# Regrouping attention products, rounded sums on GpSimd and first weights on two queues in a fp32 hybrid trunk

## The chip, the cores and the metric

The kernel runs on one core of a Trainium2 chip. The metric is the device time of one execution in microseconds (us); the median of several runs stands for the kernel. All numbers of the input and the output are fp32.

## The reference

The reference is a trunk of two layers on a sequence of 512 tokens of width 1024. Each layer mixes tokens, adds the scaled input, normalizes, and then does the same with a convolutional feed-forward network (FFN). Layer 0 mixes with a gated delta rule (GDN, six heads of 128) and a dilated sliding-window attention (SWA, three groups of four heads of 64); layer 1 with a differential attention and gated linear attention (GLA, four heads).

```python
def step(state, inp):                                  # gated delta rule, per chunk
    delta = u_n - einsum('bhck,bhkv->bhcv', w_n, state)
    o_n = einsum(qd_n, state) + einsum('bhij,bhjv->bhiv', qk_n, delta)
    state = gl_n[..., None, None] * state + einsum(kd_n, delta)
o_a = rms_norm(o_a, norm_w) * silu(z_a)
...
s = einsum(qb, kb) * dh ** -0.5 + bias                  # dilated branch, per group
p = exp(s - max(s)); o = (p / sum(p)) @ vb; lse = max + log(sum)
o = sum over the three groups of softmax(lse) * o
...
o_n = einsum(q_n * exp(b_n), state) + einsum('bhij,bhjv->bhiv', attn, v_n)   # GLA, per chunk
```

## The kernel before

**Products.** A big fp32 product (projections, FFN, output) is made of three products of rounded parts: a high part in the type fp32r and the rest ('lo'), x_hi w_hi + x_lo w_hi + x_hi w_lo, each a TensorE instruction on a 128 x 128 weight tile and 512 columns. ACT casts the weight's high part ('wh<-wr'), DVE subtracts the rest ('wl<-wr,wh'). Small products of the mixers are plain fp32, for which TensorE executes two instructions each.

**Order.** The core's engines each work through a queue in order. In the mixers the order is made by a planner: projections go out in a fixed sequence (EVEN_SEQ, L90), and between each three of their matmuls (`tile_of`, L371; `by_token`, L397) `poll` may let one of several generators ("chains") issue its next step. A chain gives control back with `yield`; the planner charges each step with rough durations per engine and holds a chain until its result should be there (`issue`). A `yield FREE` makes the chain ready once TensorE's part of the step is done. All small operations issued through the chains carry line L159 in the trace; they are told apart by the names of their tiles.

**What the change touches.**
- START (L93) is the order of the first DMA transfers: eight pieces of the input x on SyncE's queue (SP), and between them pieces of the first two weight units (0 is the narrow gate unit U_AB, 1 the first projection) on ACT's queue. In `setup` (from L221) ACT issues all five weight pieces in program order after a copy of one column (tile 'idle') that loads ACT's function table; the casts of x and of the first weights follow.
- `Scratch` (L166) hands out working tiles of 128 x 512; a tile is allocated when it is first asked for.
- `gdn_chunks` (L1157): for each head and each of four chunks, the state product, the output 'o', its square 'sq' (ACT), 'sq' plus the term 'dt' (GpSimd), its rounded copy 'hi' (ACT, L1198), and the rest 'lo' (GpSimd, L1199). 'hi' and 'lo' later go into the product that gives the mean of squares (`gdn_mean`, tile 'pm').
- `swa_pair` (L1247), for each of two pairs of heads: score products (64 rows deep) into a PSUM tile 'sps' of their own each, a reduction on DVE that adds the bias and takes the maximum, control given back after each; the maxima transposed ('rows', 'pmx'), combined over the groups and negated ('negm', 24 columns); all 24 exponentials on ACT; then, group by group, the transposes of the probabilities ('pt') and the value products into 'po' (128*64 in the trace, "PV" below), control given back after each of four blocks.
- `gla_pair`, the loop that fills 'po': for each chunk the product of 'qe' with the state (64 rows) and the product of the attention 'ats' with v (128 rows).

PSUM tiles for these small products come from a pool of four.

Of the kernel before, what the change touches and what calls it, by code (L numbers as in the profile page):

```python
# [9 lines left out]
F32 = mybir.dt.float32  # L10
# [7 lines left out]
P = 128  # L18
S = 512
# [39 lines left out]
for _n, _w in (("ident", 128), ("maskT", 128), ("nm1", 32), ("i32", 32), ("lm", 4 * 32), ("scan", 512),  # L59
# [30 lines left out]
EVEN_SEQ = "h0 h1 h2 h3 h4 h5 q00 v0 q01 v1 q02 v2 q10 q11 q12 z0 z1 z2 z3 z4 z5"  # L90
ODD_SEQ = "0D12G3abcd"

START = (("x", 0, 1), (0, 0, 4), ("x", 1, 2), (1, 0, 2), ("x", 2, 3), (1, 2, 5), ("x", 3, 4), (0, 4, 8), ("x", 4, 5),  # L93
         ("x", 5, 6), (1, 5, 8), ("x", 6, 7), ("x", 7, 8))
WARM = 8
LEAD = 3
AHEAD = 2
# [68 lines left out]
class Scratch:  # L166


    def __init__(self, t, pool, n, more=None):
        self.t, self.pool, self.free, self.of = t, pool, list(range(n)), {}  # L170
        if more is not None:
            self.free += [(k, more) for k in range(more.shape[1])]

# [21 lines left out]
class Trunk:  # L195
# [14 lines left out]
    def setup(self):  # L210
        nc, tc, ctx = self.nc, self.tc, self.ctx
        self.keep = ctx.enter_context(tc.tile_pool(name="keep", bufs=1))
        self.wp = ctx.enter_context(tc.tile_pool(name="wp", bufs=1))
        self.psd = ctx.enter_context(tc.tile_pool(name="psd", bufs=4, space=PSUM))
        self.pss = ctx.enter_context(tc.tile_pool(name="pss", bufs=4, space=PSUM))
        keep = self.keep
        self.h = keep.tile([P, KD, S], F32, name="h")
        self.xh = keep.tile([P, KD, S], F32R, name="xh")
        self.xl = keep.tile([P, KD, S], F32R, name="xl")
        first = [(u, self.wtiles()) for u in (U_AB, U_AB + 1)]  # L220

        self.ones = keep.tile([P, P], F32, name="ones")
        nc.gpsimd.memset(self.ones, 1.0 / P)
        idle = keep.tile([P, 1], F32, name="idle")
        tc.keep_in_program_order(nc.scalar.copy(out=idle, in_=self.ones[:, 0:1]))
        for what, a, e in START:
            if what == "x":
                nc.sync.dma_start(self.h[:, a, :], self.xt[:, a, :])
            else:

                u, w = first[what]
                n = 64 if u in NARROW else P
                tc.keep_in_program_order(nc.scalar.dma_start(w[0][:, a * n : e * n], self.wts[u][:, a * n : e * n]))
        self.par = keep.tile([P, _NP], F32, name="par")
        self.con = keep.tile([P, _NCC], F32, name="con")

        warm = self.sps("warm")
        for _ in range(WARM):
            nc.tensor.matmul(warm[:, 0:P], lhsT=self.ones, rhs=self.ones, start=True, stop=True)
        self.onesL = keep.tile([P, P], F32, name="onesL")  # L240
        nc.gpsimd.memset(self.onesL, 1.0 / D)
        self.onesP, self.onesK = (keep.tile([P, P], F32R, name=f"ones{i}") for i in "PK")
        for x, n in ((self.onesP, P), (self.onesK, 512)):
            nc.vector.tensor_scalar(out=x, in0=self.ones, scalar1=P / n, scalar2=None, op0=ALU.mult)
        self.cst = keep.tile([P, 3], F32, name="cst")
        self.one, self.lneps, self.gdneps = (self.cst[:, i : i + 1] for i in range(3))
        nc.gpsimd.memset(self.one, 1.0)
        nc.gpsimd.memset(self.lneps, LN_EPS)
        self.rep = tc.dram_tile([4, P, L_TAB], F32, name="rep")
        self.chains, self.rec, self.asked = [], [], {}  # L250
        self.V, self.A = Eng(self, "DVE", nc.vector), Eng(self, "ACT", nc.scalar)
        self.G, self.T = Eng(self, "POOL", nc.gpsimd), Eng(self, "PE", nc.tensor)
        self.enter(EVEN)
        for what, a, e in START:
            if what == "x":
                hi, lo = self.xh[:, a, :], self.xl[:, a, :]
                nc.scalar.copy(out=hi, in_=self.h[:, a, :])
                nc.vector.tensor_tensor(out=lo, in0=self.h[:, a, :], in1=hi.bitcast(F32), op=ALU.subtract)
            else:
                u, w = first[what]  # L260
                self.split(u, *w, nc.scalar, nc.vector, slice(a * P, e * P))
        for u, w in first:
            self.pre[u] = w[1:]
        for u in (U_AB + 2, U_AB + 3):
            self.ask(u)
        nc.sync.dma_start(self.par, self.par_d)
        nc.sync.dma_start(self.con, self.con_d)
        self.ident = self.c("ident")
# [483 lines left out]
    def even(self):  # L752
# [8 lines left out]
        def t1(n, w, bufs):  # L761
            return mp.tile([P, w], F32, name=self.nm(n), tag=n, bufs=bufs)

        self.enter(EVEN)
        g = {"zero": t1("zero", 1, 1)}
        seq = EVEN_SEQ.split()
# [390 lines left out]
    def gdn_chunks(self, hd, kt, cols, xf, ready, g, o, t1):  # L1157
# [15 lines left out]
        for c in range(NCH):  # L1173
# [21 lines left out]
            A.activation(out=ch(sq, c), in_=po, func=AF.Square)  # L1195
            st = sn

            G.tensor_tensor(out=ch(sq, c), in0=ch(sq, c), in1=ch(g["dt"][hd], c), op=ALU.add)  # L1198
            A.copy(out=ch(hi, c).bitcast(F32R), in_=ch(sq, c))  # L1199
            G.tensor_tensor(out=ch(lo, c).bitcast(F32R), in0=ch(sq, c), in1=ch(hi, c), op=ALU.subtract)  # L1200
            yield 0
        X.put(xf, vp, kt, kd, de, at, qe, sq)
# [44 lines left out]
    def swa_pair(self, pair, taken, vts, bg, o, mp, t1):  # L1247
# [12 lines left out]
        for g in range(3):  # L1260
            while len(taken) < 2 * g + 2 or X.room() < 5 or not self.bias:
                yield None
            q, k = taken[2 * g : 2 * g + 2]
            for hh in range(2):
                r = slice(64 * hh, 64 * hh + 64)
                hd = 2 * pair + hh
                tiles = []
                for n in range(NCH):
                    w = 256 if g == 0 and n > 0 else P
                    if n == 0 or (g == 0 and n == 2):  # L1270
                        while X.room() < 1:
                            yield None
                        x = X.get("sc")
                        held.append(x)
                        off = 0
                    dst = x[:, off : off + w]
                    off += w
                    bias = bg[0][:, hd, 256 - w : 256] if g == 0 else bg[g][:, hd, :]
                    k0 = n * P + P - w
                    ps = self.sps("sps")  # L1280
                    if g == 0:
                        m = max(0, 256 - w)
                        self.scores(ps[:, : w + m], q, k, hh, slice(n * P, (n + 1) * P), slice(k0, k0 + w + m))
                    else:
                        T.matmul(ps[:, :w], lhsT=q[r, n * P : (n + 1) * P], rhs=k[r, k0 : k0 + w], start=True, stop=True)
                    ci = hh * 12 + g * NCH + n
                    V.tensor_tensor_reduce(out=dst, in0=ps[:, :w], in1=bias, scale=0.125, scalar=-3e38,
                                           op0=ALU.add, op1=ALU.max, accum_out=mx[:, ci : ci + 1])
                    tiles.append((dst, k0, w))
                    yield FREE  # L1290
                sc[g, hh] = tiles
            X.put(*(q + k[0] + k[1] if g == 0 else [q, k]))

        def rows(cols, rw):

            pr = self.sps("rows")
            T.transpose(out=pr[0:24, 0:P], in_=cols, identity=self.ident)
            tr = t1("tr", P, 2)
            V.tensor_copy(out=tr[0:24, :], in_=pr[0:24, 0:P])
            for hh in range(2):  # L1300
                G.dma_start(rw[hh : hh + 1, :], tr[12 * hh : 12 * hh + 12, :])
# [12 lines left out]
        combine(rw, ALU.max, mrow)  # L1314
        yield 0
        pm = self.sps("pmx")
        for g in range(3):
            for n in range(NCH):
                src = perm(mrow[0:2, :])[:, n, :] if g else mrow[0:2, n * P : (n + 1) * P]
                T.transpose(out=pm[:, (g * NCH + n) * 2 : (g * NCH + n) * 2 + 2], in_=src, identity=self.ident[0:2, 0:2])  # L1320
        X.put(mrow)
        nm = t1("negm", 24, 2)
        V.tensor_scalar(out=nm, in0=pm[:, 0:24], scalar1=-1.0, scalar2=None, op0=ALU.mult)
        ls = t1("ls", 24, 2)
        for g in range(3):
            for hh in range(2):
                for n in range(NCH):
                    ci = (g * NCH + n) * 2 + hh
                    li = hh * 12 + g * NCH + n
                    dst, k0, w = sc[g, hh][n]  # L1330
                    A.activation(out=dst, in_=dst, func=AF.Exp, bias=nm[:, ci : ci + 1], accum_out=ls[:, li : li + 1])
                yield 0 if g == 0 and hh == 1 else FREE
        po = self.sps("po")
        for g in range(3):
            while len(vts[g]) < 2:
                yield None
            pts = {}
# [19 lines left out]
            for n in range(NCH):  # L1357
                for i in range(len(pts[0, n])):
                    for hh in range(2):
# [4 lines left out]
                        else:  # L1364
# [1 line left out]
                        vt, f = (vts[g][pair], kb * P) if g else (vts[g][kb // 2], kb % 2 * HS + P * pair)  # L1366
                        T.matmul(dst, lhsT=vt[:, f + 64 * hh : f + 64 * hh + 64], rhs=src,
                                 start=(g == 0 and n == 0 and i == 0), stop=(g == 2 and n == NCH - 1))
                yield FREE
            X.put(*temps)  # L1370
        X.put(*held)
        if pair:
# [172 lines left out]
    def gla_pair(self, pr, cs, qk, vts, gm, o, t1, done):  # L1545
# [122 lines left out]
        yield 0  # L1668
        for hh in range(2):
            po = self.sps("po")  # L1670
            for n in range(NCH):
                if n:
                    T.matmul(ch(po, n), lhsT=qe[rr[hh], n * P : (n + 1) * P], rhs=sts[n][rr[hh]], start=True, stop=False)
                T.matmul(ch(po, n), lhsT=ch(ats[hh], n), rhs=ch(vt[n], 2 * pr + hh), start=(n == 0), stop=True)
            ss = t1("gss", NCH, 4)
            for n in range(NCH):
                A.activation(out=ch(ats[hh], n), in_=ch(po, n), func=AF.Square, accum_out=ss[:, n : n + 1])
# [325 lines left out]
```

## Time and profile before

| | before |
|---|---|
| median of 3 runs | 1410.34 us (1410.32 to 1410.57) |
| the profiled execution | 1412.89 us |
| its span in the trace | 1411.1 us |
| stages in the trace (us) | start 0 to 18; even mixer 18 to 374; its output product 374 to 430; FFN 430 to 798; odd mixer 798 to 1004; its output product 1004 to 1045; FFN 1045 to 1411 |

The profile was taken in one execution on the chip. PE is TensorE's matmul, DVE VectorE, ACT ScalarE, POOL GpSimd, SP SyncE. L12 is line 12 of the kernel; `out<-in` are the program's names of the tiles. In the timelines a row is: start, duration, engine, line, operation, tiles, shape, count of instructions in a row, and in brackets the idle time before with what ended it. Matmuls are pipelined, so that their durations overlap; the distance of two starts says how long one occupies the engine.

### The profile page before, as it was taken

The numbers are of one execution on the slowest core, as the hardware profiler recorded it, in microseconds if no ns is written. First come the engines' busy times: TensorE is split into PE (matmuls) and PEld (weight loads), VectorE is DVE, ScalarE is ACT, GpSimd is POOL, SyncE is SP. The second block draws the span as 40 slices with busy tenths as digits, with TensorE's granted clock in tenths as the row PEclk, the third lists the DMA queues.
The fourth block names the chain that finished last, engine by engine and source line by source line (L and its number), as shares of the span: only waits on it lengthen the run. The fifth ranks groups of instructions, "written<-read, shape, count | busy, mean of one in ns | idle before, by whom it ended". The sixth has DMA issues, their size and how long they took to land.

```text
span 1411.1 us, 22721 instructions
## 1 busy us (share of the span) xinstructions
PE 1385.7 (98%) x9050; PEld 1151.2 (82%) x9050; DVE 839.3 (59%) x1635; ACT 673.5 (48%) x1285; POOL 179.8 (13%) x237
## 2 busy tenths in 40 slices
PE   8999999999999999999999999999999999999997
PEld 6878787777798888888888977878898888888886
DVE  6876744544586555555243797777776555553354
ACT  6644433644857344434132755557565344432133
POOL 2103012011023111111010310000131111110010
PEclk9999999999999999999999999999999999999998
DMA  7434112121342322323233313211303322223221
GB/s 248 144 111 149 47 61 75 36 73 61 98 128 76 99 95 97 98 95 100 96 98 98 88 61 105 75 46 60 120 31 119 99 96 95 99 95 100 91 73 60
DMA packets 41457, 130.42 MB, mean 92 GB/s; under 512 B 4637, under 2 KB 9485, under 8 KB 41352
## 3 DMA queue, kind: packets, MB, share of 16 engines
q1 hardware_dynamic: 35584, 119.05, 26.1%
q10 hardware_dynamic: 4184, 4.92, 1.2%
q0 software_dynamic: 1584, 5.00, 1.1%
q8 instruction: 71, 1.16, 0.3%
q14 instruction: 34, 0.28, 0.1%
HBM read 126.76 MB, written 5.29 MB: 94 GB/s over the span
## 4 chain that ended last, share of the span: by engine, by line
PE 83%; DVE 6%; ACT 5%; DMA 3%; issue 2%; POOL 1%; ACTq 0%; DVEq 0%; POOLq 0%
PE pd L487 18%; PE pd L488 18%; PE pd L489 17%; PE pd L371 16%; PE pd L397 3%; DMA wr<-wts 2%; PE pc L159 1%; PE po L159 1%; PE sps L159 1%; PE pz L159 1%; PE py L159 1%; PE pa L159 1%; PE dsc L159 1%; DVE wl L159 1%; PE dpo L159 1%
## 5 line engine op out<-in xcount | busy, mean ns | idle before, releaser
L500 DVE TENSOR_TENSOR wl<-wr,wh 128x1024 fp32r<-128x1024 f32 (+1 forms) x153 | 187.9, 1229 | 301.8 <-ACT wh L499 298.7
L488 PE MATMUL pd<-xl,wh 128*128 128x512 f32 (+1 forms) x968 | 353.6, 366 | 0.2 <-DVE xl L684 0.2
L487 PE MATMUL pd<-xh,wh 128*128 128x512 f32 (+1 forms) x968 | 353.1, 366 | 0.4 <-ACT xh L683 0.4
L489 PE MATMUL pd<-xh,wl 128*128 128x512 f32 (+1 forms) x968 | 353.1, 365 | 0.0
L499 ACT CAST wh<-wr 128x1024 fp32r<-128x1024 f32 (+1 forms) x156 | 159.8, 1030 | 196.7 <-PE pd L488 171.4
L487 PEld LDWEIGHTS pd<-xh,wh 128*128 128x128 f32 x968 | 182.4, 189 | 30.4 <-ACT xh L683 0.9
L488 PEld LDWEIGHTS pd<-xl,wh 128*128 128x128 f32 x968 | 182.6, 189 | 30.1 <-DVE xl L684 1.1
L489 PEld LDWEIGHTS pd<-xh,wl 128*128 128x128 f32 x968 | 182.7, 189 | 29.5 <-issue 0.8
L371 PE MATMUL pd<-xh,wh 128*128 128x512 f32 x424 | 172.7, 407 | 0.0
L371 PE MATMUL pd<-xl,wh 128*128 128x512 f32 x424 | 170.9, 403 | 0.0
L487 PE MATMUL pd<-ah,wh 128*128 128x512 f32 (+1 forms) x396 | 145.1, 366 | 0.0
L489 PE MATMUL pd<-ah,wl 128*128 128x512 f32 (+1 forms) x396 | 144.7, 366 | 0.0
L488 PE MATMUL pd<-al,wh 128*128 128x512 f32 (+1 forms) x396 | 144.7, 365 | 0.0
L721 DVE SCALAR_TENSOR_TENSOR y<-pd,par,y 128x510 f32<-128x510 f32 (+1 forms) x176 | 130.4, 745 | 2.8
L371 PE MATMUL pd<-xh,wl 128*128 128x512 f32 x424 | 117.8, 402 | 0.0
L730 POOL TENSOR_TENSOR al<-y,ah 128x512 fp32r<-128x512 f32 x44 | 59.1, 1343 | 407.6 <-ACT ah L729 407.6
L159 DVE TENSOR_TENSOR wl<-wr,wh 128x1024 fp32r<-128x1024 f32 x63 | 77.1, 1224 | 42.6 <-PE pd L371 17.6
L159 ACT CAST wh<-wr 128x1024 fp32r<-128x1024 f32 x63 | 65.9, 1047 | 66.6 <-PE pd L371 48.2
L371 PEld LDWEIGHTS pd<-xl,wh 128*128 128x128 f32 x424 | 80.5, 190 | 16.2 <-issue 1.9
L371 PEld LDWEIGHTS pd<-xh,wh 128*128 128x128 f32 x424 | 80.4, 190 | 15.7 <-issue 0.3
L371 PEld LDWEIGHTS pd<-xh,wl 128*128 128x128 f32 x424 | 76.4, 188 | 14.6 <-issue 0.7
L487 PEld LDWEIGHTS pd<-ah,wh 128*128 128x128 f32 x396 | 74.7, 189 | 12.2
(387 smaller groups left out, 1868.6 us busy)
## 6 DMA issues: line engine op xcount, KB each, us to landing
wr<-wts SPq DMA_DIRECT2D x213, 512.0 KB, 3.4
h<-xt SPq DMA_DIRECT2D x16, 256.0 KB, 4.1
rep<-tab POOLq DMA_DIRECT2D x1, 3072.0 KB, 15.5
h<-gd POOLq DMA_DIRECT2D x6, 256.0 KB, 7.5
qe<-ge ACTq DMA_DIRECT2D x5, 256.0 KB, 4.4
bd<-rep ACTq DMA_DIRECT2D x1, 1024.0 KB
out<-h SPq DMA_DIRECT2D x2, 512.0 KB, 3.2
con<-con SPq DMA_DIRECT2D x1, 544.0 KB
```

Of the source, the lines that this page charges most:

```text
L159: r = fn(*a, **k)
L371: self.nc.tensor.matmul(ps, lhsT=w[part][:, k * P : (k + 1) * P], rhs=x[:, k, :], start=(i == 0), stop=(i == 23))
L397: self.nc.tensor.matmul(pss[b][:, a : a + n], lhsT=chunk(x[:, k, :], c), rhs=ws, start=(k == 0 and a == 0 and not part and x is self.xh), ...
L487: nc.tensor.matmul(ps, lhsT=wh, rhs=ah, start=first, stop=False)
L488: nc.tensor.matmul(ps, lhsT=wh, rhs=al, start=False, stop=False)
L489: nc.tensor.matmul(ps, lhsT=wl, rhs=ah, start=False, stop=last)
L499: A.copy(out=hi, in_=raw)
L500: V.tensor_tensor(out=lo, in0=raw, in1=hi.bitcast(F32), op=ALU.subtract)
L721: V.scalar_tensor_tensor(out=y[:, sft:], in0=ps[:, : S - sft], scalar=w(2 - sft), in1=y[:, sft:], op0=ALU.mult, op1=ALU.add)
L730: G.tensor_tensor(out=al[:, f, :], in0=y, in1=ah[:, f, :].bitcast(F32), op=ALU.subtract)
```

## The change

- START is reordered: U_AB now in pieces 0:2, 2:5 and 5:8, alternating with unit 1's; the first three weight pieces (FIRST = 3) go out on ACT's queue, the other three on SP's between pieces of x.
- The tile 'idle' goes; 'cst' is allocated earlier with 32 columns and takes its place, and 'par' is padded to a multiple of 32 columns. `Scratch` allocates all its tiles at once, and the state tiles st0 to st3 are allocated at the start of the even mixer.
- In `gdn_chunks`, GpSimd writes the rounded sum 'hi' itself with a second add (fp32r output) in place of ACT's copy.
- In `swa_pair`, groups 1 and 2 issue the four score products of a head at once into one PSUM tile (ps4); 'pmx' has 8 transposes in place of 12 and 'negm' 16 columns; the exponentials of group 0 and 1 come before PV of group 0, those of group 2 before PV of group 1; control is given back after each group's PV in place of each block's; 'tr' has one buffer.
- In `gla_pair`, the three 64-row products of a head come first, then the four 128-row ones.

```diff
-START = (("x", 0, 1), (0, 0, 4), ("x", 1, 2), (1, 0, 2), ("x", 2, 3), (1, 2, 5), ("x", 3, 4), (0, 4, 8), ("x", 4, 5),
-         ("x", 5, 6), (1, 5, 8), ("x", 6, 7), ("x", 7, 8))
+START = (("x", 0, 1), (0, 0, 2), ("x", 1, 2), (1, 0, 2), ("x", 2, 3), (0, 2, 5), ("x", 3, 4), (1, 2, 5), ("x", 4, 5),
+         (0, 5, 8), ("x", 5, 6), (1, 5, 8), ("x", 6, 7), ("x", 7, 8))
+FIRST = 3
...
+        for i in range(n):
+            pool.tile([P, S], F32, name=t.nm("x"), tag=f"x{i}", bufs=1)
...
-        idle = keep.tile([P, 1], F32, name="idle")
-        tc.keep_in_program_order(nc.scalar.copy(out=idle, in_=self.ones[:, 0:1]))
-        for what, a, e in START:
+        self.cst = keep.tile([P, 32], F32, name="cst")
+        tc.keep_in_program_order(nc.scalar.copy(out=self.cst[:, 8:9], in_=self.ones[:, 0:1]))
+        for i, (what, a, e) in enumerate(START):
...
-                tc.keep_in_program_order(nc.scalar.dma_start(w[0][:, a * n : e * n], self.wts[u][:, a * n : e * n]))
-        self.par = keep.tile([P, _NP], F32, name="par")
+                here = i < 2 * FIRST
+                d = (nc.scalar if here else nc.sync).dma_start(w[0][:, a * n : e * n], self.wts[u][:, a * n : e * n])
+                if here:
+                    tc.keep_in_program_order(d)
+        self.par = keep.tile([P, -(-_NP // 32) * 32], F32, name="par")[:, :_NP]
...
+        for i in range(4):
+            t1(f"st{i}", P, 2)
...
-            G.tensor_tensor(out=ch(sq, c), in0=ch(sq, c), in1=ch(g["dt"][hd], c), op=ALU.add)
-            A.copy(out=ch(hi, c).bitcast(F32R), in_=ch(sq, c))
+            qq = ch(g["dt"][hd], c)
+            G.tensor_tensor(out=ch(hi, c).bitcast(F32R), in0=ch(sq, c), in1=qq, op=ALU.add)
+            G.tensor_tensor(out=ch(sq, c), in0=ch(sq, c), in1=qq, op=ALU.add)
             G.tensor_tensor(out=ch(lo, c).bitcast(F32R), in0=ch(sq, c), in1=ch(hi, c), op=ALU.subtract)
...
+                if g:
+
+                    ps4 = self.sps("sps")
+                    for n in range(NCH):
+                        b = slice(n * P, (n + 1) * P)
+                        T.matmul(ps4[:, b], lhsT=q[r, b], rhs=k[r, b], start=True, stop=True)
...
-                        T.matmul(ps[:, :w], lhsT=q[r, n * P : (n + 1) * P], rhs=k[r, k0 : k0 + w], start=True, stop=True)
+                        ps = ps4[:, n * P : (n + 1) * P]
...
-        for g in range(3):
+        for g in range(2):
             for n in range(NCH):
                 src = perm(mrow[0:2, :])[:, n, :] if g else mrow[0:2, n * P : (n + 1) * P]
                 T.transpose(out=pm[:, (g * NCH + n) * 2 : (g * NCH + n) * 2 + 2], in_=src, identity=self.ident[0:2, 0:2])
...
-        nm = t1("negm", 24, 2)
+        nm = t1("negm", 16, 2)
...
-        for g in range(3):
+
+        def exps(g):
...
-                    ci = (g * NCH + n) * 2 + hh
+                    ci = (min(g, 1) * NCH + n) * 2 + hh
...
+        yield from exps(0)
         po = self.sps("po")
         for g in range(3):
+            if g < 2:
+                yield from exps(g + 1)
...
-                yield FREE
+            yield FREE
             X.put(*temps)
...
+            for n in range(1, NCH):
+                T.matmul(ch(po, n), lhsT=qe[rr[hh], n * P : (n + 1) * P], rhs=sts[n][rr[hh]], start=(n == 1), stop=False)
             for n in range(NCH):
-                if n:
-                    T.matmul(ch(po, n), lhsT=qe[rr[hh], n * P : (n + 1) * P], rhs=sts[n][rr[hh]], start=True, stop=False)
-                T.matmul(ch(po, n), lhsT=ch(ats[hh], n), rhs=ch(vt[n], 2 * pr + hh), start=(n == 0), stop=True)
+                T.matmul(ch(po, n), lhsT=ch(ats[hh], n), rhs=ch(vt[n], 2 * pr + hh), start=False, stop=(n == NCH - 1))
```

## Rows read from the trace of the kernel before

**Rows 1.** The page: busy time by engine (share, instructions), and the chain's shares.
```profile
PE 1385.7 (98%) x9050; PEld 1151.2 (82%) x9050; DVE 839.3 (59%) x1635; ACT 673.5 (48%) x1285; POOL 179.8 (13%) x237
...
PE 83%; DVE 6%; ACT 5%; DMA 3%; issue 2%; POOL 1%; ACTq 0%; DVEq 0%; POOLq 0%
```
**Rows 2.** Windows: stretch, length, busy PE, PEld, DVE, ACT, POOL, granted clock, DMA share, GB/s.
```profile
18.00:374.00 356.00, 348.18 (x3598) 280.94 (x3596) 211.76 (x552) 183.61 (x452) 48.57 (x100) 1.00 0.27 87
...
430.00:798.00 368.00, 367.86 (x1768) 310.29 (x1768) 193.53 (x250) 152.42 (x218) 52.55 (x52) 1.00 0.29 95
...
30.00:34.00 4.00, 4.00 (x13) 3.10 (x12) 2.68 (x5) 2.43 (x5) 2.66 (x5) 0.61 0.27 70
```
**Rows 3.** Timeline of PE, projection matmuls; the first and the last of seven starts.
```profile
25.62 0.39 PE L371 MATMUL pd<-xh,wh 128*128 128x512 f32 x1
...
26.98 0.84 PE L371 MATMUL pd<-xh,wl 128*128 128x512 f32 x3
```
**Rows 4.** Timeline of PE, GLA's output loop.
```profile
937.97 0.48 PE L159 MATMUL po<-gs,qe 64*128 64x128 f32 x2
938.38 0.49 PE L159 MATMUL po<-vt,ga 128*128 128x128 f32 x2
```
**Rows 5.** Timeline of PE, fp32 products of one shape behind each other.
```profile
203.45 0.39 PE L159 MATMUL pc<-at,de 128*128 128x128 f32 x2
203.67 0.39 PE L159 MATMUL pc<-qe,st 128*128 128x128 f32 x2
```
**Rows 6.** Timeline of PE, score products among projection matmuls.
```profile
242.73 0.48 PE L159 MATMUL sps<-sq,sq 64*128 64x128 f32 x2
243.15 1.20 PE L371 MATMUL pd<-xh,wl 128*128 128x512 f32 x4
244.28 0.48 PE L159 MATMUL sps<-sq,sq 64*128 64x128 f32 x2
```
**Rows 7.** Timeline of PE, the matmuls before and after PV products of pair 0.
```profile
275.42 0.39 PE L371 MATMUL pd<-xh,wh 128*128 128x512 f32 x1
...
276.87 0.39 PE L371 MATMUL pd<-xh,wl 128*128 128x512 f32 x1
```
**Rows 8.** The chain of work: start, time, engine, tile, line.
```profile
259.87 1.34 PE pmx L159 x12
```
**Rows 9.** Timeline of ACT, two casts of the squares' high part.
```profile
141.97 0.30 ACT L159 CAST hi<-sq 128x128 fp32r<-128x128 f32 x1 [1.67 <-POOL sq L159]
...
222.29 0.30 ACT L159 CAST hi<-sq 128x128 fp32r<-128x128 f32 x1 [2.96 <-POOL sq L159]
```
**Rows 10.** Waits of PE: waiting tile, releaser, sum in us, how many, longest.
```profile
PE pvt L159 <- ACT vf L159: 1.7, 1, 1.7
PE pg L159 <- ACT wh L159: 1.5, 1, 1.5
PE pkk L159 <- DVE kd L159: 1.4, 1, 1.4
```
**Rows 11.** Timeline of GpSimd, 134 to 137 us.
```profile
134.52 0.46 POOL L159 TENSOR_TENSOR sq<-sq,dt 128x128 f32<-128x128 f32 x1 [3.75 <-ACT sq L159]
135.38 1.14 POOL L159 TENSOR_TENSOR lo<-sq,hi 128x128 fp32r<-128x128 f32 x1 [0.41 <-ACT hi L159]
```
**Rows 12.** Timeline of DVE, the same stretch.
```profile
134.98 1.23 DVE L159 TENSOR_TENSOR wl<-wr,wh 128x1024 fp32r<-128x1024 f32 x1 [0.41 <-PE pd L371]
```
**Rows 13.** Timeline of PE at the start.
```profile
7.16 0.79 PE L507 MATMUL pd<-xh,wh 128*128 128x512 f32 x1 [2.37 <-DVE wh L500]
```
**Rows 14.** Timeline of ACT at the start.
```profile
5.42 0.62 ACT L257 CAST xh<-h 128x512 fp32r<-128x512 f32 x1 [3.19 <-DMA h<-xt]
...
17.30 1.05 ACT L159 CAST wh<-wr 128x1024 fp32r<-128x1024 f32 x1 [1.14 <-DMA wr<-wts]
```
**Rows 15.** Timeline of ACT in the mixer's tail.
```profile
367.00 0.93 ACT L159 COPY pt<-pt 128x512 f32<-128x512 f32 x2
```
**Rows 16.** Timeline of ACT, the copy of a mean of squares.
```profile
336.50 0.59 ACT L159 COPY dt<-pm 128x512 f32<-128x512 f32 x1 [8.71 <-PE pm L159]
```

More of the change, by code (lines that the diff above doesn't have):

```diff
@@ L244, in setup @@
             nc.vector.tensor_scalar(out=x, in0=self.ones, scalar1=P / n, scalar2=None, op0=ALU.mult)
-        self.cst = keep.tile([P, 3], F32, name="cst")
         self.one, self.lneps, self.gdneps = (self.cst[:, i : i + 1] for i in range(3))
@@ L1279, in swa_pair @@
                     k0 = n * P + P - w
-                    ps = self.sps("sps")
                     if g == 0:
+                        ps = self.sps("sps")
                         m = max(0, 256 - w)
@@ L1297, in rows @@
             T.transpose(out=pr[0:24, 0:P], in_=cols, identity=self.ident)
-            tr = t1("tr", P, 2)
+            tr = t1("tr", P, 1)
             V.tensor_copy(out=tr[0:24, :], in_=pr[0:24, 0:P])
@@ L1321, in swa_pair @@
         X.put(mrow)
-        nm = t1("negm", 24, 2)
-        V.tensor_scalar(out=nm, in0=pm[:, 0:24], scalar1=-1.0, scalar2=None, op0=ALU.mult)
+        nm = t1("negm", 16, 2)
+        V.tensor_scalar(out=nm, in0=pm[:, 0:16], scalar1=-1.0, scalar2=None, op0=ALU.mult)
         ls = t1("ls", 24, 2)
-        for g in range(3):
+        def exps(g):
             for hh in range(2):
                 for n in range(NCH):
-                    ci = (g * NCH + n) * 2 + hh
+                    ci = (min(g, 1) * NCH + n) * 2 + hh
                     li = hh * 12 + g * NCH + n
```

## The prediction, made before the changed kernel ran

> **What bounds the kernel now.** I read the page's busy shares and its chain of work first. TensorE (PE) is busy 98% of the span and carries 83% of the chain that ended last; DVE is at 59%, ACT at 48%, GpSimd (POOL) at 13% [rows 1]. So an edit is worth what it takes out of PE's own sequence, or out of the few holes in it. The table of windows says where these are: in the first FFN (430 to 798 us) PE is idle 0.14 of 368 us, and the change touches nothing there; in the even mixer (18 to 374 us) it is idle 7.82 of 356 us [rows 2]. Then PE's timeline, for what its small products cost beside their work, and the list of waits for the holes. The unit: six projection matmuls with 512 columns start between 25.62 and 26.98 us, 0.227 us each [rows 3]. PE's busy time hides the slack I look for, since the modelled durations overlap; I count from start to start.
>
> **Four scores together, GLA products by shape (path).** In GLA's output loop 64-row and 128-row products alternate. Each is two instructions (fp32), and a step from one product to the next, shape changed, takes 0.41 to 0.42 us (937.97 to 938.38) [rows 4]. Where fp32 products of one shape follow each other the step is 0.22 us (203.45 to 203.67) [rows 5]. So a change of shape costs 0.195 us. The loop has seven products with six changes inside; after it, three 64-row ones and then four 128-row ones: one change inside and one at entry, four fewer. It runs four times (two pairs of heads, two heads each): 4 x 4 x 0.195 = **3.1 us**. Upper bound 4.0 if the entry costs nothing.
>
> The Trainium skill ("TensorEngine Tiling (Array Packing)", Key Properties) says that a switch of the tiling mode drains the array; the 0.195 us of these rows agrees.
>
> Scores of attention groups 1 and 2 are issued one by one, 64 rows deep, among 128-row projection matmuls. From 242.73 to 244.28 us lie one score and four projection matmuls: 1.55 us, of which 4 x 0.227 and 2 x 0.11 are work; 0.42 is the price of a visit [rows 6]. PE's timeline of 204 to 247 and 328 to 336 us has 15 visits (of 2 to 10 instructions). Four products per group and head become one visit: groups 1 and 2 of four heads make at most eight, seven fewer, 7 x 0.42 = **3.0 us** (rounded up for products of unequal wait; 2.3 if two visits of group 0 split, 4.5 if neighbours merge). DVE's four reductions now read one PSUM tile; they hold it 4 x longer, and the next tile comes from the same pool of four, so up to 0.4 us per group could come back; that is inside the 2.3.
>
> **PV by group (path, half).** The value products of pair 0 fall in seven visits, 275.73 to 297 us, because the generator gives control back after every block. One of them, with twelve half-width instructions in six pairs, takes 275.42 to 276.87, 1.45 us, with two projection matmuls: 1.45 - 2 x 0.227 - 6 x 0.11 = 0.34 [rows 7]. Three visits after the change: 4 x 0.34 = **1.3 us**. In pair 1 four visits lie in the mixer's tail, where PE waits for ACT; 0 there.
>
> **Fewer transposes.** The twelve 'pmx' transposes take 1.34 us, 0.11 each; the negated maxima of groups 1 and 2 have equal columns, and the change keeps eight [rows 8]. PE is alone there, in each pair: 2 x 4 x 0.11 = **0.9 us**. (DVE's scaling of 16 instead of 24 columns: 0.)
>
> **Squares' high part on GpSimd.** Removed: 24 ACT casts of 0.30 us, 7.2 us of ACT. What they really cost is where they wait: a cast sits in ACT's in-order queue until GpSimd has added, and GpSimd may be held by a DMA of its own; ACT stood 1.67 us before the cast at 141.97 and 2.96 before that at 222.29 [rows 9]. What is queued behind it feeds PE: PE waits 1.4 us for 'kd' (DVE, after ACT's reductions) and 1.7 us for 'vf' (ACT) right after these two places [rows 10]. After the change ACT's next work in the queue waits for no GpSimd result. Of 3.1 us I take **2.7 us**, as other work is then late by some tenths; bounds 1.0 (only one goes) and 3.1.
>
> Added: 24 adds of 0.46 us on GpSimd, 11 us [rows 11]. The chain per chunk becomes add, add, subtract (1.4 us) in place of add, ACT's cast with two handovers, subtract (0.46 + 0.41 + 0.46): about equal. Nothing on PE reads 'hi' and 'lo' before the mean product, which follows several chunks later; taken as 0. GpSimd is held while DVE splits weights: the subtract at 135.38 took 1.14 us [rows 11] beside DVE's split at 134.98 [rows 12]. If every added instruction were so, 24 x 1.14 = 27 us on GpSimd, whose 48 us in 356 leave room [rows 2].
>
> Here the Trainium skill speaks against the change: "GPSIMD Engine Reference", Engine selection, gives elementwise two-input work to VectorE, and "SBUF — State Buffer", in its section on the two sides, has GpSimd and VectorE lock one port pair against each other. The 1.14 against 0.46 us agrees with the lock. By it the sum would be the slower rival below.
>
> **First weights on two queues.** PE's first projection starts at 7.16 us after 2.37 us of waiting [rows 13]; ACT's first cast stands 3.19 us until 5.42, with its five DMA issues ahead [rows 14]. With three issues there the cast can come up to 1.9 us sooner. But the second unit's weights land at 17.28 us regardless (ACT waits 1.14 us for them) [rows 14], all transfers share the same bytes, and PE then stands 1.5 us at the gate product whose chain begins there [rows 10]. A sooner start lengthens that stand: gain **0**, bounds 0 and 3.2: the 1.5 us, plus 1.7 us if the stretch that follows (0.61 granted over 30 to 34 us, mostly the lower level of 1.2 GHz [rows 2]) goes too. The three pieces moved to SP are queued between x pieces: on SP nothing else waits so early.
>
> **Exponentials by group.** Same instructions in another order. In the tail ACT works on without a break, and PE waits for it: the last 'pt' copies start at 367.00 [rows 15]. With ACT's sum unchanged the end stays; taken 0, bounds 1.3 either way (one wait of PE there, or one table load). **Aligned and preallocated tiles, padding:** no instruction changes; 0, within 1.
>
> **The sum.** 3.1 + 3.0 + 1.3 + 0.9 + 2.7 = 11.0 us. The profiled execution took 1412.89 us (span 1411.1, 1.8 around it), 2.5 above the median of 1410.34; the terms are differences within it and are taken off the median: 1410.3 - 11.0 = **1399.3 us**.
>
> **Rivals.** (A) *The start counts too.* If the gate chain does come earlier because ACT and SP issue its weights sooner, 1.5 to 3.2 us more: about 1396. For it: the half-clock stretch follows a hole, so removing the hole removes both. Against: the DMA share is at its full value until 16 us, and no byte is saved.
> (B) *The planner gives some back.* The hand-written schedule charges a chunk's step by its instructions, and three GpSimd adds are charged longer than ACT's cast; the mean product of the last heads comes later and its consumers meet the tail. ACT already stood 8.71 us before the copy of such a mean at 336.50 [rows 16]. Exponentials that now alternate with other work can also make ACT change its function table once more per pair. Price some 2 x 1.3 + 2 = 4.6: about 1404.
> (C) *It doesn't do what it says.* The visits of scores are spread by the waits on DVE, not by issue, and stay 15; the ACT holds go to another cast. Only GLA and pmx count, 4.0 us: 1406.4.
> (D) *Slower.* One mechanism: GpSimd's queue becomes the path. Each chunk now has three two-input operations on GpSimd, at 0.46 us free and 1.14 beside DVE's splits [rows 11]; decays ('qe') and the state's copies for the next head stand behind them in the same queue, and PE waits for those. At 1.14 us 24 added instructions are 27 us. It decides from the point where over 40% of them (11 us) lie on the path. If 60% do, 16 us against 11: about 1415. For it: the 2.96 us at 222.29 is already a wait for GpSimd. Against: GpSimd works 48 us of 356, and DVE's splits coincide with few of its instructions (one of 20 subtracts took over 1 us).
>
> **How the numbers follow.** Forecast 1399.3 (1396.5 to 1402.5 by its bounds): 0.58. A 0.12, B 0.14, C 0.08, D 0.08. The range 8 in 10 takes in A, the bounds of the forecast and most of B and a part of C: 1394.5 to 1407.0. Two tenths of a percent, 2.8 us, is about what a measurement of this kernel tells from no change. Faster by more: forecast, A, B and most of C, 0.83 with a little off each; within: 0.09 (B and C at their worst); slower: D with part of B, 0.08.
>
> **What would show it.** In the trace of after: GLA's products in two runs, the seven taking about 1.8 us in place of 2.6; scores of groups 1 and 2 in visits of eight instructions; 'pmx' x8; no wait of ACT for 'sq' of GpSimd, and no hole of PE before 'pkk' and 'pvt'; the FFNs unchanged to 0.2 us; the gate product at about 29.3 us still. The forecast is wrong if PE has new holes in 120 to 374 us whose releaser is GpSimd or the mean, if a table load more appears in 340 to 374, or if the first gate product moves by over 1 us.

## The result and the profile after

| | before | after |
|---|---|---|
| median | 1410.45 us (1410.32 to 1410.70) | 1426.21 us (1425.70 to 1426.84) |
| ratio | | 1.0112, interval 1.0094 to 1.0129 |
| the profiled execution's span | 1411.1 us | 1423.9 us |

The change makes the kernel 15.8 us slower where 11 us less were forecast; the time lies outside the range of 1394.5 to 1407.0 us. Line numbers of the kernel after are 1 to 22 higher (the helper is L160, the FFN's products L494 to L496).

The page of after, busy time by engine, answers to [rows 1]: PE has 8 matmuls fewer (the transposes), and yet 9.9 us more busy time. ACT lost twenty instructions, GpSimd got 24.

```profile
PE 1395.6 (98%) x9042; PEld 1152.5 (81%) x9042; DVE 842.0 (59%) x1636; ACT 672.0 (47%) x1265; POOL 195.0 (14%) x261
```

The same stages read off PE's timelines show where the time went. Starts of matmuls in us; the last column is how much later a stage ends than before, and of that the part that the stage adds:

| stage ends with | before | after | later (added) |
|---|---|---|---|
| last projection of the even mixer | 364.95 | 356.17 | -8.8 (-8.8) |
| first output product of layer 0 | 373.93 | 378.69 | +4.8 (+13.5) |
| first down product of FFN 0 | 663.46 | 674.03 | +10.6 (+5.8) |
| first projection of the odd mixer | 802.30 | 812.86 | +10.6 (0.0) |
| first output product of layer 1 | 982.89 | 991.07 | +8.2 (-2.4) |
| first down product of FFN 1 | 1276.74 | 1289.99 | +13.3 (+5.1) |
| last down product of FFN 1 | 1398.77 | 1411.99 | +13.2 (0.0) |

Two things stand out. The two FFNs' first halves, which the diff does not touch, take 5 to 6 us more each (in the table together with the output product ahead of them), and their second halves nothing. And PE is through with the even mixer's projections 9 us sooner, but its tail, from there to the first output product, grew by 13.5 us.

PE's timeline in FFN 0 of after (start, duration): seven steps in 1.63 us, 233 ns each, where [rows 3] had 227. Over the stretch from 450 to 650 us the mean step is 232.4 ns, before 226.7.

```profile
499.75 0.39 PE L494 MATMUL pd<-xh,wh 128*128 128x512 f32 x1
...
501.38 0.39 PE L495 MATMUL pd<-xl,wh 128*128 128x512 f32 x1
```

The groups of lines by shape (count, busy us, mean ns of one; idle before) put a number on it: products that read xh have a mean of 395 ns in after, those that read ah in the FFN's second half 389.

```profile
L494 PE MATMUL pd<-xh,wh 128*128 128x512 f32 x744 | 292.8, 395 | 0.0
L494 PE MATMUL pd<-ah,wh 128*128 128x512 f32 x308 | 119.8, 389 | 0.0
```

The mixer's tail in after: waits of PE, longest first, to be held against [rows 10] (the waits for 'vf' and 'kd' are gone; there is a new one of 7.2 us).

```profile
PE po L160 <- DVE h L160: 7.2, 1, 7.2
PE py L160 <- DVE uu L160: 2.1, 2, 1.1
PE pt L160 <- ACT sc L160: 1.7, 3, 1.1
```

ACT's timeline of after in the same stretch, five of its table loads:

```profile
352.86 1.28 ACT L420 ACT_TABLE_LOAD   x1
361.07 1.28 ACT L160 ACT_TABLE_LOAD   x1
362.98 1.28 ACT L160 ACT_TABLE_LOAD   x1
368.32 1.28 ACT L160 ACT_TABLE_LOAD   x1
370.23 1.28 ACT L160 ACT_TABLE_LOAD   x1
```

DVE's timeline of after: DVE waits 5.34 us for ACT in the normalization of the GDN's output, and the copies of 'pt' that PE waits for stand behind that in DVE's queue.

```profile
358.49 0.75 DVE L160 SCALAR_TENSOR_TENSOR o<-o,par,dt 128x512 f32<-128x512 f32 x1 [5.34 <-ACT dt L160]
...
363.08 1.15 DVE L160 COPY h<-pt 128x512 f32<-128x512 f32 x2
```

From 340 us to the output product ACT loads a table seven times, before four times. In the window from 357 to 380 us (columns as in [rows 2]) ACT is busy 22.86 of 23 us, and PE 14.08. PE's granted clock is 0.70 there, that is in part 1.2 GHz; in PE's timeline, below it, PV pairs that took 0.11 us take 0.21.

```profile
357.00:380.00 23.00, 14.08 (x83) 10.09 (x84) 12.81 (x21) 22.86 (x57) 1.00 (x2) 0.70 0.06 16
```
```profile
370.35 0.42 PE L160 MATMUL po<-pt,vt 128*64 128x128 f32 x1
...
370.56 0.42 PE L160 MATMUL po<-pt,vt 128*64 128x128 f32 x1
```

### The profile page after: what moved, and what is told of

It reads as the page before. It is cut to its first block, busy times and chain, and to the rows that moved or that the text cites. A ratio compares the mean times of both kernels' runs of the same rounds, so it can differ in the third digit from the quotient of the medians.

```text
span 1423.9 us, 22717 instructions
## 1 busy us (share of the span) xinstructions
PE 1395.6 (98%) x9042; PEld 1152.5 (81%) x9042; DVE 842.0 (59%) x1636; ACT 672.0 (47%) x1265; POOL 195.0 (14%) x261
## 4 chain that ended last, share of the span: by engine, by line
PE 84%; DVE 7%; ACT 4%; issue 3%; DMA 1%; POOL 0%; ACTq 0%; SPq 0%; DVEq 0%; POOLq 0%
PE pd L494 18%; PE pd L495 18%; PE pd L496 18%; PE pd L378 16%; PE pd L404 3%; PE pc L160 2%; PE po L160 1%; PE pz L160 1%; PE py L160 1%; PE dsc L160 1%; PE pa L160 1%; PE sps L160 1%; PE dpo L160 1%; DVE h L160 1%; DVE xx L160 1%
## 5 line engine op out<-in xcount | busy, mean ns | idle before, releaser
L496 PE MATMUL pd<-xh,wl 128*128 128x512 f32 (+1 forms) x968 | 356.6, 369 | 0.0
L494 PE MATMUL pd<-xh,wh 128*128 128x512 f32 (+1 forms) x968 | 356.3, 370 | 0.0
L506 ACT CAST wh<-wr 128x1024 fp32r<-128x1024 f32 (+2 forms) x157 | 159.6, 1022 | 220.1 <-PE pd L495 183.7
L496 PEld LDWEIGHTS pd<-xh,wl 128*128 128x128 f32 x968 | 182.5, 189 | 33.2 <-issue 0.8
L494 PEld LDWEIGHTS pd<-xh,wh 128*128 128x128 f32 x968 | 182.2, 189 | 33.4 <-ACT xh L690 0.4
L494 PE MATMUL pd<-ah,wh 128*128 128x512 f32 (+1 forms) x396 | 145.1, 366 | 0.0
L496 PE MATMUL pd<-ah,wl 128*128 128x512 f32 (+1 forms) x396 | 144.7, 365 | 0.0
L160 DVE TENSOR_TENSOR wl<-wr,wh 128x1024 fp32r<-128x1024 f32 x63 | 78.1, 1239 | 51.1 <-PE pd L378 21.4
L160 ACT CAST wh<-wr 128x1024 fp32r<-128x1024 f32 x63 | 65.7, 1045 | 84.4 <-PE pd L378 48.3
L495 PEld LDWEIGHTS pd<-al,wh 128*128 128x128 f32 x396 | 74.7, 189 | 12.2
## 6 DMA issues: line engine op xcount, KB each, us to landing
rep<-tab POOLq DMA_DIRECT2D x1, 3072.0 KB, 15.8
```

The lines of the kernel that those rows point to most:

```text
L160: r = fn(*a, **k)
L494: nc.tensor.matmul(ps, lhsT=wh, rhs=ah, start=first, stop=False)
L495: nc.tensor.matmul(ps, lhsT=wh, rhs=al, start=False, stop=False)
L496: nc.tensor.matmul(ps, lhsT=wl, rhs=ah, start=False, stop=last)
L506: A.copy(out=hi, in_=raw)
```

## The experiments

### Where the tiles lie

The trace gives no addresses; the places are counted from the program, in bytes of each partition, with tiles rounded up to 32 bytes. In the pool 'keep', x's parts (16384 each), 'ones' (512), 'idle' (32), 'par' (1984), 'con' (4352), three more tiles of constants (512 each) and 'cst' (32) lie between the start of xh and the first weight tile: 2 x 16384 + 512 + 32 + 1984 + 4352 + 1536 + 32 = 41216 bytes, 161 x 256. The change makes 'cst' 128 bytes, 'par' 2048 and drops 'idle': 128 bytes more. Everything behind moved by 128 bytes against x: the weights, and also ah and al, the high part and the rest of what the FFN's second half reads. Theory 1 was that this slows the products on x; the runs undo the move, make it alone in the kernel before, and make it for x as well.

```diff
         self.con = keep.tile([P, _NCC], F32, name="con")
+        keep.tile([P, 32], F32, name="gap")
```

In the changed kernel (a1):

> The changed kernel with an unused tile of 32 columns (128 bytes per partition) at the end of the pool 'keep', so that the weight tiles and all later pools start 128 bytes further on. Theory 1 (place of the tiles): in the changed kernel projection matmuls that read xh or xl start 232.4 ns apart in the FFNs, before 226.7; the padding of 'par' and 'cst' put the weights at a multiple of 256 bytes while x lies 128 bytes off one. Shifted back, all of them return to 226.7 ns: 2112 matmuls of the two FFNs and 384 of the output products x 5.7 ns = 14.2 us, and some 2 to 4 us in the mixers: 1408 to 1410 us. Rival (the order of work or GpSimd's adds slow the matmuls): 232 ns and 1426 us stay.

Measured: 1412.57 us (1410.84 to 1414.84), 13.6 less than after; the ratio to before is 1.0008 (0.9999 to 1.0017). The matmuls are back: from 450 to 650 us 226.7 ns a step, and 390 ns in the group.

```profile
L495 PE MATMUL pd<-xh,wh 128*128 128x512 f32 x744 | 288.6, 390 | 0.0
```

In the kernel before (b1), and ahead of 'h' there (c1: the same line in front of self.h):

> The kernel before with the same unused 128 bytes at the end of 'keep' ('tr' has one buffer, as in the changed kernel, to make room). Theory 1: weights at a multiple of 256 bytes make the matmuls on xh and xl 232 ns apart without any other part of the change: 1410.4 + 16 to 18 = 1426 to 1429 us, and the FFN's second half (on ah, al), which moves along with the weights, stays at 226.7 ns. Rival: 1410 us.

> The kernel before with the unused 128 bytes at the front of 'keep', so that x and the weights move together ('tr' has one buffer, to make room). Theory 1a (what counts is the distance of x and the weights, both streams being read at once): 226.7 ns and 1410 us. Theory 1b (what counts is the weights' own place at a multiple of 256 bytes): 232 ns, 1426 to 1429 us.

Measured: b1 1425.88 us, 1.0098 (1.0082 to 1.0114); c1 1411.02 us, 0.9996 (0.9986 to 1.0005). So 128 bytes that no instruction reads make the kernel before as slow as the whole change did, and only if x and the weights don't move together. The group of b1, then that of c1:

```profile
L488 PE MATMUL pd<-xh,wh 128*128 128x512 f32 x744 | 293.5, 396 | 0.4 <-ACT xh L684 0.4
L488 PE MATMUL pd<-ah,wh 128*128 128x512 f32 x308 | 119.9, 389 | 0.0
```
```profile
L488 PE MATMUL pd<-xh,wh 128*128 128x512 f32 x744 | 289.5, 391 | 0.4 <-ACT xh L684 0.4
```

The crossed case (e1) moves the weights by 128 bytes against both x and ah:

```diff
+        keep.tile([P, 32], F32, name="gap")                # behind 'con': weights +128
...
+        ctx.enter_context(tc.tile_pool(name="gp", bufs=1)).tile([P, 32], F32, name="gap2")   # behind the pool of the weights
```

> The changed kernel with 128 unused bytes ahead of the weight tiles and 128 more behind them, so that only the weights change their place modulo 256 bytes, and all later pools keep theirs. If the distance between the two streams that TensorE reads is what counts, products on xh and xl return to 226.7 ns, and the FFN's second half on ah and al, until now 226.7, goes to 232: 13.6 us less for x, 1188 x 5.7 = 6.8 us more (estimate by those that have 512 columns: 924 x 5.7 = 5.3): 1418 to 1420 us. If the place of other tiles (those that ACT, DVE and GpSimd write meanwhile) is what counts, the products on x stay at 232 and the time at 1426; if the weights' place alone does, ah and al stay at 226.7 and the time is 1412 to 1413.

Measured: 1419.05 us (1417.55 to 1420.21). The slow half of the FFN changed sides, xh 390 ns and ah 395. Apart from the weight tiles, which serve both halves, every tile that DVE, ACT and GpSimd write lies where it lay in after, so the places of those are not it.

```profile
L496 PE MATMUL pd<-xh,wh 128*128 128x512 f32 x744 | 288.9, 390 | 0.0
L496 PE MATMUL pd<-ah,wh 128*128 128x512 f32 x308 | 121.7, 395 | 0.0
```

How the loss goes with the distance (8, 16 and 48 columns in place of 32, in the kernel before):

> The kernel before with 32 unused bytes ahead of the weights ('tr' has one buffer, to make room): the distance from x to the weights is 32 bytes past a multiple of 256, before 0, in the changed kernel 128. If every distance that is no multiple of 256 bytes costs: about 232 ns between matmuls and 1425 us. If only the neighbourhood of 128 does: 226.7 ns and 1411 us.

> The same with 64 bytes. If every distance but a multiple of 256 costs: 232 ns. If the loss grows with the distance up to 128: about 229 ns and 1418 us. If only 128 counts: 226.7 ns.

> The same with 192 bytes. If the loss goes by the distance to the nearest multiple of 256, as 64 bytes does; if it goes by the half of 256 bytes in which a tile begins, as 128 bytes does: 232 ns, 1425 us.

Measured, one execution each: 1425.92, 1427.09 and 1416.55 us beside 1414.66 for the kernel before in the same session (its median elsewhere is 1410.5, so that the times say less here than the steps between matmuls). Steps in FFN 0 from 450 to 650 us: 233.3 ns at 32 bytes, 233.3 at 64, 233.3 at 128 (b1), 228.9 at 192, 226.7 at 0 and at 256 (a1). For 32 and 64 bytes the first case expected came true, for 192 neither did: every distance tried that is no multiple of 256 bytes costs, but not by the distance to the nearest multiple; 192 costs a third of what 64 does. Two things limit this. The slow step has two values at one distance: at 128 bytes b1 takes 233.3 ns in FFN 0 and 232.4 in FFN 1, after 232.4 in both. And products of x with 256 columns take no longer: from 412 to 436 us their step is 120.0 ns in before, 118.8 in after, 119.3 in b1. Group of 64 bytes, then of 192:

```profile
L488 PE MATMUL pd<-xh,wh 128*128 128x512 f32 x744 | 294.0, 397 | 0.4 <-ACT xh L684 0.4
```
```profile
L488 PE MATMUL pd<-xh,wh 128*128 128x512 f32 x744 | 292.1, 394 | 0.4 <-ACT xh L684 0.4
```

### The mixer's tail

With the exponentials ahead of the first PV, as before the change (d1 on the changed kernel, f1 with the 128 bytes as well):

```diff
-        yield from exps(0)
+        for g in range(3):
+            yield from exps(g)
         po = self.sps("po")
         for g in range(3):
-            if g < 2:
-                yield from exps(g + 1)
```

> The changed kernel with all 24 exponentials ahead of the first PV again, everything else as changed. Theory 2: the exponentials by group alternate on ACT with the z gates' function in the mixer's tail; seven table loads from 347 to 376 us in place of four before, 3 x 1.28 = 3.8 us on ACT, which ends the tail: 1422 us, and PE's wait of 7.2 us for DVE's copies shrinks. Rival: the tail is bound by the order on DVE (the copies of PV behind the output's scaling), not by the loads: 1426 us.

> The changed kernel with both repairs: the unused 128 bytes that bring the weights back to the distance from x that they had before, and all exponentials ahead of the first PV. If the two costs add up, 1426.2 - 13.6 - 5.3 = 1407.3 us, 0.997 of before, of which GLA's 3 us are the larger part. If the forecast's terms for the mixer (scores 3.0, PV 1.3, transposes 0.9, GpSimd 2.7) also come through: 1399 to 1401 us. The rival, that the mixer's tail is paced by ACT whatever PE saves ahead of it, gives 1407.

Measured: d1 1420.88 us (5.3 less than after), f1 1408.74 us, 0.9983 (0.9975 to 0.9992). The price of the grouping is there, but not mainly as table loads: d1 has six from 340 us where after has seven, which is 1.3 us of the 5.3. In d1 the negated maxima ('negm'), at which ACT's tail begins, come at 341.1 us instead of 347.7: the other sequence of steps made the planner issue the maxima's chain sooner. The tail from there to the output product is equally long (30.5 and 31.0 us). Before, 'negm' came at 348.2 us: of the 8.8 us by which PE was sooner in after, only 0.5 reached the start of ACT's tail, and the tail itself was 5.3 us longer than before (25.8). f1's mixer still ends at 372.4 us, 1.5 sooner than before: some 6 of the forecast's 7.9 us for it were missing.

Two undo parts of the change on f1:

> The kernel with both repairs, but the squares' high part is ACT's cast again, as before. By the forecast's term (ACT no longer held behind GpSimd) it is 2.7 us slower than with both repairs alone, with PE's waits before 'pkk' and 'pvt' back. If the tail absorbs what PE gains ahead of it: within 1 us. If the GpSimd adds cost time: faster.

> The kernel with both repairs, but each score product of groups 1 and 2 is issued by itself into a PSUM tile of its own. By the forecast's term 3.0 us slower than with both repairs alone (seven more visits at 0.42 us). If the planner now lets several chains step between two projection matmuls, so that visits were never as many as counted, under 1 us.

```diff
-            G.tensor_tensor(out=ch(hi, c).bitcast(F32R), in0=ch(sq, c), in1=qq, op=ALU.add)      # g1
             G.tensor_tensor(out=ch(sq, c), in0=ch(sq, c), in1=qq, op=ALU.add)
+            A.copy(out=ch(hi, c).bitcast(F32R), in_=ch(sq, c))
...
-                        ps = ps4[:, n * P : (n + 1) * P]                                          # h1
+                        ps = self.sps("sps")
+                        T.matmul(ps[:, :w], lhsT=q[r, n * P : (n + 1) * P], rhs=k[r, k0 : k0 + w], start=True, stop=True)
```

Measured: h1 1411.58 us, 1.0001 (0.9992 to 1.001): 2.8 us more than f1 by the medians. Visits of scores: 12 in h1, 5 in f1, 15 before. In the two profiled executions the mixers end alike (372.0 and 372.4 us), so where the 2.8 us lie is not shown.

g1 1403.13 us, 0.9939 (0.9926 to 0.9953): ACT's cast back is 5.6 us *faster*, against the forecast's term of 2.7 the other way, although PE's waits for 'vf' (1.7 us) and 'kd' (1.4), which are gone in f1, are back. The traces show what differs: the last GDN mean reaches ACT at 339.49 us in g1, ahead of the maxima (340.98), and at 346.48 in f1, after ACT has begun the exponentials. ACT then loads a table for the output's roots (347.06), one for a z gate ('h<-pd', 355.29) and one to get back to the exponentials (357.20). f1's timelines, of ACT and of DVE:

```profile
341.44 1.28 ACT L160 ACT_TABLE_LOAD   x1
...
346.48 0.56 ACT L160 COPY h<-pm 128x512 f32<-128x512 f32 x1
347.06 1.28 ACT L421 ACT_TABLE_LOAD   x1
...
355.29 1.28 ACT L160 ACT_TABLE_LOAD   x1
356.58 0.60 ACT L160 ACTIVATE h<-pd 128x512 f32<-128x512 f32 x1
357.20 1.28 ACT L160 ACT_TABLE_LOAD   x1
```
```profile
342.06 0.17 DVE L160 TENSOR_SCALAR negm<-pmx 128x16 f32<-128x16 f32 x1 [2.32 <-PE pmx L160]
```

A mean behind the maxima is not new, though. Before, it reached ACT at 352.13 us, 4 us after the maxima, but the exponentials went on behind the roots without another load, with no z gate between (before, ACT and then DVE):

```profile
352.13 0.56 ACT L159 COPY h<-pm 128x512 f32<-128x512 f32 x1
352.71 1.28 ACT L413 ACT_TABLE_LOAD   x1
...
360.83 0.39 ACT L159 ACTIVATE sc<-sc,negm 128x128 f32<-128x128 f32 x1
...
367.95 1.28 ACT L159 ACT_TABLE_LOAD   x1
```
```profile
348.17 0.18 DVE L159 TENSOR_SCALAR negm<-pmx 128x24 f32<-128x24 f32 x1 [1.38 <-PE pmx L159]
```

Theory 3: it is not the adds, but that the planner charges three GpSimd adds otherwise than an add, a cast and an add, and places the mean by GpSimd's booked time. l1 keeps the change's GpSimd adds and books the step as before:

```diff
-            G.tensor_tensor(out=ch(hi, c).bitcast(F32R), in0=ch(sq, c), in1=qq, op=ALU.add)
+            G.eng.tensor_tensor(out=ch(hi, c).bitcast(F32R), in0=ch(sq, c), in1=qq, op=ALU.add)   # not booked
             G.tensor_tensor(out=ch(sq, c), in0=ch(sq, c), in1=qq, op=ALU.add)
+            self.rec.append(("ACT", A.time("copy", (), {"out": ch(hi, c)})))                      # booked as the cast
```

> The kernel with both repairs (weights back at their distance from x, exponentials first), GpSimd writing the squares' high part as in the change, but the planner books that step as before the change (ACT's cast between two GpSimd adds), so that TensorE's and DVE's order is that of the kernel with ACT's cast. Theory 3 (the planner: three GpSimd adds are charged longer, the last mean is issued after the exponentials have begun, and ACT changes tables more): the time is that of the kernel with ACT's cast or better, 1400 to 1403.5 us, the 2.7 us of the forecast at most coming on top. Rival (the adds themselves cost on GpSimd, by its queue or by DVE): 1407 to 1409 us.

Measured: 1401.65 us (1398.67 to 1402.55), 0.9928 (0.9915 to 0.9942), 7.1 us less than f1 and the lowest median of all. The bookings alone are thus worth 7.1 us. With the same adds on GpSimd, the mean is at ACT by 338.25 us, ahead of the maxima (339.75), and the roots run before the exponentials. Of ACT's loads one is saved, since the exponentials follow under the roots' table; the two around the z gates stay (350.82 and 353.22). The output product starts at 366.68 us, in f1 at 372.42 (l1's timelines of ACT and of DVE).

```profile
338.25 0.59 ACT L160 COPY h<-pm 128x512 f32<-128x512 f32 x1 [0.54 <-PE pm L160]
338.86 1.28 ACT L421 ACT_TABLE_LOAD   x1
...
350.82 1.28 ACT L160 ACT_TABLE_LOAD   x1
...
353.22 1.28 ACT L160 ACT_TABLE_LOAD   x1
...
361.64 1.28 ACT L160 ACT_TABLE_LOAD   x1
...
366.33 1.28 ACT L421 ACT_TABLE_LOAD   x1
```
```profile
339.75 0.17 DVE L160 TENSOR_SCALAR negm<-pmx 128x16 f32<-128x16 f32 x1 [0.60 <-PE pmx L160]
```

Three more have ACT's cast and the 128 bytes: m1 with the exponentials by group; n1 and o1 with them first, n1 with START as before (FIRST = 7, all on ACT's queue), o1 with control given back after each block of PV.

> The changed kernel with the weights back at their distance from x and ACT's cast of the high part; the exponentials stay by group. If the groups' order costs its table loads in any case: 1403.1 + 4 = 1407 us, six or more loads from 340 us to the mixer's end. If it cost only because the last mean came late: 1403 us.

> Both repairs and ACT's cast, with the order and the queues of the first weight pieces as before the change. By the forecast's term 0: 1403 us. Rival: the first projection starts 0.9 us later (7.1 instead of 6.2 to 6.5 us), the gate product 1.5 us later, and that reaches the end: 1404 to 1405 us.

> Both repairs and ACT's cast, with control given back after each block of value products as before the change. By the forecast's term (four more visits in pair 0 at 0.34 us) 1.3 us slower than 1403.1; if the tail after pair 1 is paced by ACT and takes up what pair 0 gained: 1403.

Measured: m1 1404.75 us, 0.9958 (0.9946 to 0.9971); n1 1402.78 us, 0.9946 (0.9934 to 0.9959); o1 1403.81 us, 0.9950 (0.9937 to 0.9962). m1 falls between its two cases: six loads from 340 us (g1 five), but only 1.6 us over g1, in overlapping intervals. The grouping's own price is thus small or none with ACT's cast and its bookings. START is worth nothing that can be measured, PV by group 0.7 us at most, within the intervals.

## Why the prediction was wrong

Three steps lead from after to l1: 13.6 us for the place of the tiles (after to a1), 3.8 for the sequence of exponentials (a1 to f1), 7.1 for the planner's bookings (f1 to l1). l1, the change without these three, lies 9.0 us below the kernel before, of the 11.0 forecast. That 13.6 + 3.8 + 7.1 - 9.0 = 15.5 us meets the measured 15.8 proves nothing, since each step is the difference of two neighbours; and the sizes depend on the order of the steps: with ACT's cast the grouping costs 1.6 us in place of 3.8.

- **Aligned and preallocated tiles, 0 within 1.** This step failed, and it is half of the miss of 26.9 us (1426.2 against 1399.3). Its reason was that no instruction changes. The instructions did not; their pace did, by 5.7 ns for each product of x with 512 columns in FFN 0, since 128 bytes of padding changed the distance between the two operands that TensorE reads. The three lines of these products (L494 to L496) hold 744 each, 2232 in all, which makes 12.7 us; the profiled executions of after and a1 differ by 12.4 us in their spans. The 14.2 us expected for a1 counted as 512 columns wide what in part has 256 and does not get slower. The change makes 'par' and 'cst' multiples of 128 bytes, and that took away the multiple of 256 that the tiles happened to have. There was no rival with a longer matmul, and the prediction's own sign of being right, the FFNs unchanged to 0.2 us, failed. The Trainium skill ("SBUF — State Buffer", section on the two sides) says that TensorE never waits for anyone on the engines' side; that sentence is about other engines, and no run here tests it. What b1, c1 and e1 show is a cost that hangs on the two operands of TensorE itself.
- **Squares on GpSimd, 2.7 gained, rival B 4.6 given back.** The forecast priced a queue and took the planner as a rival of 0.14. The wait at 'kd' went as forecast; the one at 'vf' went in after and f1 but not in l1 (1.8 us), so ACT's hold behind GpSimd does not explain it alone. On the chip the adds are worth 1.5 us (l1 against g1), within the intervals. The forecast's error is the planner's share: B named it, with the dearer booking and extra loads, but at 4.6 us; measured are 3.8 and 7.1, 10.9 us together. The mean is not later than before (352.3 us in after, 352.1 before); it misses the earlier place that the old bookings give it (338.3 in l1). From 'negm' to the output product ACT's tail takes 25.8 us before, 30.4 in f1 and 26.9 in l1. The roots' place and the extra loads account for part of that; why the tail of before is so short with its mean as late was not tested apart.
- **Exponentials by group, 0 within 1.3.** Wrong with the change's bookings (3.8 and 5.3), nearly right with ACT's cast (1.6, within the intervals). The argument "the same instructions" forgot that another sequence of yields is another plan.
- **GLA, 3.1.** Right: from the odd mixer's first projection to its output product it is 177.6 us in a1, 180.6 before; the other runs of the changed kernel with x and the weights at their old distance lie between 177.3 and 178.3. The seven products come in two runs of one shape each (951.28 to 953.14 us, 1.9 us, where the forecast said 1.8), PE's timeline of after:

```profile
951.28 0.93 PE L160 MATMUL po<-gs,qe 64*128 64x128 f32 x6
952.15 1.16 PE L160 MATMUL po<-vt,ga 128*128 128x128 f32 x8
```

- **Scores 3.0, transposes 0.9, PV 1.3, start 0.** Scores: five visits, not eight; 2.8 us by undoing them. Transposes: 0.89 us each time in place of 1.34 [rows 8], 0.9 in all. PV: three visits in pair 0 as forecast (g1), 0.7 us in the undoing, not apart from nothing. Start: 0 by the times (n1), but not for the reason given, which was that the gate product stays at about 29.3 us. It came at 27.86 us in after, with a wait of PE of 0.7 us in place of 1.5; n1, whose gate product comes 1.1 us later than g1's, is no slower.
- **Rival D.** The kernel is slower, as D said, but by 15.8 us and not by 5, and for another reason. GpSimd's queue does not set the path: with all 24 adds on it, l1 has the lowest median, and they cost GpSimd 10.4 us of busy time (191.4 in l1, 181.0 in g1), not 27. The Trainium skill ("GPSIMD Engine Reference", Engine selection) gives such adds to VectorE. No run here did that; on GpSimd they cost nothing that can be measured, so there was little to save.

## What to carry to other kernels

Padding, a dropped scratch tile or a new constant moves every tile behind it: compare the operands' distance modulo 256 bytes before and after, and the step between equal matmuls in a stage that the diff does not touch. Where a schedule is planned from booked costs, changing the engine of one small operation changes the plan; test the operation with the old bookings before judging it. A gain of PE ahead of a tail that another engine paces counts only as far as that engine's chain begins sooner.

## What was not expected of the hardware

A 128 x 512 fp32r matmul stream takes 226.7 ns a step when moving operand and weights lie a multiple of 256 bytes apart in a partition, 233.3 at 32, 64 and 128 bytes past one (232.4 in after, also 128), and 228.9 at 192 (FFN 0, 450 to 650 us). Moving both together costs nothing (c1), and products with 256 columns take no longer. Which of TensorE's two accesses is held up, why 192 differs from 64, and why 128 has two values, stays open.
